# Where matmul operands start in on-chip memory: 512-byte lines for all of them, and contiguous stationary columns in the MLP

## The chip, the core and the metric

The kernel runs on one core of a Trainium2 chip. The metric is the device time of one execution in microseconds, as the median of several runs. TensorE (PE) multiplies; ScalarE (ACT) and VectorE (DVE) do the elementwise work; SyncE (SP) issues every DMA of the weights. SBUF is the on-chip memory from which TensorE reads both operands of a matmul: the stationary one (128 columns, loaded by a weight load, PEld) and the streamed one (256 or 512 columns here, read while the matmul runs).

## The reference, cut to what matters

A token stream of 256 tokens of width 1024 runs through two hybrid layers of one kind, then two of another. All arithmetic is float32.

```
# first kind, DEPTH = 2
h    = rmsnorm(x, pre_mix_g)
proj = h @ w_in                                    # 1024 -> 7440
y_a  = gated_delta_rule(conv_silu(q, k, v)) @ w_up_dn
y_b  = sliding_window_attention(...) @ w_up_sw
x    = x + rmsnorm((sigmoid(gate_a) * y_a + sigmoid(gate_b) * y_b) @ w_o, post_mix_g)
h2   = rmsnorm(x, pre_mlp_g)
x    = x + rmsnorm(square(relu(h2 @ w_ff1)) @ w_ff2, post_mlp_g)     # 1024 -> 4096 -> 1024

# second kind, DEPTH = 2, on the token stream h and a context stream hc (256 x 1024 each)
m  = silu(c) @ w_ada + b_ada                       # nine modulation rows, also for the context
h  = h + 0.5 * gate * rmsnorm(swiglu(pre(h), ffn_wi[0], ffn_wo[0]))  # 1024 -> 2 x 2816 -> 1024; also hc
o  = attention mixes of (pre(h) @ w_in) and of the context
h  = h + gate * rmsnorm(o @ w_o)                   # also hc, except in the last layer
h  = h + 0.5 * gate * rmsnorm(swiglu(pre(h), ffn_wi[1], ffn_wo[1]))  # also hc, except in the last layer
```

Nearly all of it, counted in multiplications, is the products with weights: activations (256 tokens) against weight matrices that come from HBM once.

## The kernel before, in words

Float32 accuracy is made out of a reduced float32 kind (F32R): each operand is split into a high part and the rest (`split_psum` and `wtile` do it), and each product into three matmuls into one PSUM tile, high by high, high by rest, rest by high (`mm3`, lines 262 to 268: L266, L267, L268). So the matmuls of weights come in threes, on L266, L267 and L268 in turn.

`wtile` (L237) loads a weight tile: it issues the DMAs into `raw`, ScalarE writes the high part `hi`, VectorE the rest `lo`. `hi` and `lo` are made by `shifted` (L185) in the pool `W`, in three buffers each, taken in turn; a few tiles have a buffer of their own (`hi4`, `lo4`). Each buffer is 16 elements longer than its tile.

The products run in two forms.

- **Weights stationary** (`lin_b`, L388): a weight tile of 1024 rows by 256 columns. For each stream the columns are taken in two halves of 128 and for each half the 8 blocks of rows: 2 x 8 x 3 = 48 matmuls, each with 128 stationary weight columns and 256 streamed tokens of the layer's input `xT` (`xTh` of the token stream, `xTc` of the context, both split in two). In the FFN of the second kind a weight tile serves the context and then the token stream. The program has 239 such groups of 48: 146 on `xTh`, 69 on `xTc`, 8 on `oT`, and 16 on `xTh` whose results stand in PSUM tiles called `sm`.
- **Weights streamed** (`out_mm` L1038, `lin_a` L365): 128 stationary tokens of an activation (`hid`, `mT`, `xTh`, `xTc`), and 512 columns of weights, of 4 blocks of rows at a time: groups of 12 matmuls, 306 in the program. Some products have 432 or 384 columns (288 matmuls each), and 576 matmuls stream 256 columns (`by_tokens`, L1020, at the start of the MLPs).

In the MLP of the first kind (`layer1`, from L952) the argument `turns=True` gives the hidden units an order of their own: the stationary operand of a half is every second column (`slice(j, None, 2)` in `lin_b`, L396), and the rows of `w_ff2` are loaded so that partition p holds rows 2p and 2p+1 of a pair of blocks (L255 to L257). 24 of the 239 groups are of this kind (4 plus 8 in each of two layers); `back` (L1029) reads every second column as well.

The order of all instructions is that of a recording layer with priorities; each engine runs its own list in order, and the pools' buffers say which waits there are. SyncE issues the loads of weights in their order, each when its `raw` buffer is free.

Of the kernel before, what the change touches and what calls it, by code (L numbers as in the profile page):

```python
# [9 lines left out]
F32R = mybir.dt.float32r  # L10
# [7 lines left out]
P = 128  # L18
# [4 lines left out]
EPS = 1e-6  # L23
# [9 lines left out]
TAIL = 8  # L33
# [130 lines left out]
class Kern:  # L164
    def __init__(self, tc, I, out, dbg=None):
        self.tc, self.nc, self.I, self.out, self.dbg = tc, tc.nc, I, out, dbg
        self.uid = 0
        self.flip = self.nraw = self.nw = 0
        self.deferred = []
        self.credit = self.ada_rate = 0.0  # L170

# [10 lines left out]
        kw = {} if bufs is None else {"bufs": bufs}  # L182
        return pool.tile(list(shape), dt, tag=tag, name=f"{tag}_{self.uid}", **kw)

    def shifted(self, pool, kt, n, tag, by, bufs):  # L185

        flat = self.t(pool, [P, kt * n + 16], tag, F32R, bufs=bufs)
        return flat[:, by:by + kt * n].rearrange("p (k n) -> p k n", n=n)

    def dump(self, name, ap):  # L190
# [43 lines left out]
            self.stt(lo, ps, scale, hi, ALU.mult, ALU.subtract)  # L234


    def wtile(self, parts, kt, n, own=None, turns=False):  # L237

        if own is None:
            self.nw += 1  # L240
            hi, lo = (self.shifted(self.W, kt, n, x, 0, self.w_bufs) for x in ("hi", "lo"))
        else:
            hi, lo = (self.shifted(own, kt, n, x, 0, 1) for x in ("hi4", "lo4"))
        step = 1024 // n
        for k in range(0, kt, step):
            m = min(step, kt - k)
            self.nraw += 1
            if self.raw_pool and self.nraw % 4 == 0:
                raw = self.t(self.raw_pool, [P, m, n], "raw4", bufs=1)
            else:  # L250
                raw = self.t(self.W, [P, m, n], "raw", bufs=3)
            for ap, c0 in parts:
                src = ap[k * P:(k + m) * P]
                dst = raw[:, :, c0:c0 + ap.shape[1]]
                if turns:  # L255
                    dst = dst.rearrange("p (c j) n -> p c j n", j=2)
                self.nc.sync.dma_start(out=dst, in_=src.rearrange("(c p j) n -> p c j n" if turns else "(k p) n -> p k n", p=P, **({"j": 2} if turns else {})))  # L257
            self.act(hi[:, k:k + m, :], raw)
            self.tt(lo[:, k:k + m, :], raw, hi[:, k:k + m, :], ALU.subtract)
        return hi, lo  # L260
# [124 lines left out]
                self.tick(sum(h[1] for h in held) * n)  # L385
            held = []

    def lin_b(self, parts, xs, evac, w=None, tag="mm", turns=False):  # L388


        wh, wl = w or self.wtile(parts, KB, 256)
        for key, (xh, xl) in xs:
            self.need((key, 0), (key, 1))
            ps = self.psum([P, 2, 256], tag)
            for j in range(2):
                c = slice(j, None, 2) if turns else slice(j * P, (j + 1) * P)  # L396
                for k in range(KB):
                    self.mm3(ps[:, j, :], (wh[:, k, c], wl[:, k, c]), (xh[:, k, :], xl[:, k, :]), k == 0, k == KB - 1)
            evac(key, ps)
            self.tick(16 * S)  # L400
# [35 lines left out]
    def setup(self, es):  # L436
        nc, I = self.nc, self.I

        self.t(self.pool(es, "line", side="right"), [P, 8], "line")
        self.keep = self.pool(es, "keep")  # L440
        self.small = self.pool(es, "small")
        self.cst = self.t(self.keep, [P, K_END2], "cst")
        self.cols = self.t(self.keep, [P, C_END], "cols")
        self.h = Stream("h", self.t(self.keep, [P, 2, D], "xh"))
        nc.sync.dma_start(out=self.h.x[:, 0, :], in_=I["x"][0:P, :])
        self.ident = self.cst[:, K_ID:K_ID + P]
        self.one = self.cst[:, K_ONE:K_ONE + 1]
# [415 lines left out]
    def layer1(self, l, nx, last, begin):  # L863
        nc, I = self.nc, self.I
        h = self.h
        w_in = I["w_in"][l]
        with ExitStack() as es:
            mp = self.pool(es, f"mix{l}", side="right")
            self.lay = mp
            if not begin:  # L870
                self.ada_rate = RATE1
            xh, xl = nx.x["h"]
# [3 lines left out]
            with ExitStack() as es2:  # L876
                op = self.pool(es2, f"o{l}", side="right")
                oh = self.t(op, [P, KB, S], "oT", F32R, bufs=2)
                ol = self.t(op, [P, KB, S], "oT", F32R, bufs=2)
                swt = [self.t(op, [P, 1296], "swt", bufs=2) for _ in range(2)]  # L880
                def ev(key, ps, c):
                    nc.scalar.copy(swt[key[1]][:, c * 432:(c + 1) * 432], ps)

                tiles = []
                for c, k in ((0, 0), (0, 4), (1, 0), (1, 4)):
                    w_ = self.wtile([(w_in[k * P:(k + 4) * P, 4096 + 432 * c:4528 + 432 * c], 0)], 4, 432, op if c and k else None)
# [25 lines left out]
                for c in range(4):  # L912
# [2 lines left out]
                        self.stt(s, s, 1.0, ps, ALU.add, ALU.mult)  # L915
                    self.lin_b([(I["w_up_sw"][l][:, 256 * c:256 * c + 256], 0)], [("h", (oh, ol))], ev)
            rp = self.pool(es, f"rest{l}", side="right")
            ob = [self.t(rp, [P, 8, P], "ob", bufs=2) for _ in range(2)]
            zz = [self.t(rp, [P, D], "zz", bufs=2) for _ in range(2)]
            ga = self.t(rp, [P, KB, S], "ga")  # L920
# [20 lines left out]
            for tb in range(2):  # L941
# [4 lines left out]
                s = slice(tb * P, (tb + 1) * P)  # L946
# [12 lines left out]
            nx = self.norm1(pre2)  # L959
            self.out_proj(xp, I["w_o"][l], KB, self.xs_of("h", (mh, ml)), {"h": (h, self.row_bc(I["post_mix_g"][l], xp))},  # L960
                          4 * EPS, nx)
        with ExitStack() as es:
            xh, xl = nx.x["h"]
            if l < DEPTH - 1:
                nx = self.norm1(self.row_bc(I["pre_mix_g"][l + 1], self.rowp, "gpre"))
            else:
                self.close_rows()
            mp = self.raw_pool = self.pool(es, f"ff{l}", side="right")
            self.ada_rate = 0.0
            nb = D_FF // P  # L970
# [15 lines left out]
            def unit(c, tag):  # L986
                def ev(key, ps):
                    r = relu2(ps)
                    hi, lo = place(c)
                    nc.scalar.copy(hi, r)  # L990
                    self.tt(lo, r, hi, ALU.subtract)
                self.lin_b([(w1[:, 256 * c:256 * c + 256], 0)], [("h", (xh, xl))], ev, tag=tag, turns=True)


            tiles = [self.wtile([(w1[:, 256 * c:256 * c + 256], 0)], KB, 256, mp if c == 3 else None) for c in range(FIRST)]
            for tb in range(2):
                self.need(("h", tb))
                s = slice(tb * P, (tb + 1) * P)
                for c in range(FIRST):
                    r = relu2(self.by_tokens((xh, xl), s, tiles[c]))  # L1000
                    self.back(r[:, 0, :], [x[:, :, s] for x in place(c)], turns=True)
            for c in range(FIRST, nb // 4):
                unit(c, "mm")
            xs = [(("h", tb), lambda k, tb=tb: [x[:, k % 2, tb * P:(tb + 1) * P] for x in hid[k // 2]]) for tb in range(2)]
            ps = {}
            gates = {"h": (h, self.row_bc(I["post_mlp_g"][l], mp))}
            self.ada_rate = RATE1
            self.out_head(w2, 0, nb // 2, nb, xs, ps, turns=True)
            if l == DEPTH - 1:
                nx = last()  # L1010
            self.ada_rate = 0.0
            for c in range(nb // 4, nb // 2):
                unit(c, "sm")
            self.ada_rate = RATE1
            self.out_proj(mp, w2, nb, xs, gates, EPS, nx, start=nb // 2, ps=ps, turns=True)
            self.raw_pool = self.rowp if l < DEPTH - 1 else None
        return nx

# [5 lines left out]
        self.tick(KB * 256)  # L1024
        return ps

    def back(self, r, out, turns=False):

        n = r.shape[-1] // P  # L1029
        pt = self.psum([P, n, P])  # L1030
        for j in range(n):
            self.nc.tensor.transpose(pt[:, j, :], r[:, j::n] if turns else r[:, j * P:(j + 1) * P], self.ident)
        self.split_psum(out[0], out[1], pt)

    def wrows(self, w, c, k, kt, own=None, turns=False):
        return self.wtile([(w[k * P:(k + kt) * P, c * 512:(c + 1) * 512], 0)], kt, 512, own, turns)

    def out_mm(self, ps, key, get, c, k, kt, nk, w_):  # L1038
        if (key, c) not in ps:
# [1 line left out]
        for j in range(kt):  # L1041
            self.mm3(ps[key, c], get(k + j), (w_[0][:, j, :], w_[1][:, j, :]), k + j == 0, k + j == nk - 1)

    def out_head(self, w, start, end, nk, xs, ps, k0=0, turns=False):
        for c in range(2):
            for k in range(start, end, 4):
                kt = min(4, end - k)
                w_ = self.wrows(w, c, k0 + k, kt, None, turns)
                for key, get in xs:
                    self.out_mm(ps, key, get, c, k, kt, nk, w_)  # L1050
                self.tick(kt * len(xs) * 512)

    def out_proj(self, pool, w, nk, xs, gates, eps, nx, k0=0, acc=None, tail=TAIL, start=0, ps=None, turns=False):


        head = nk - tail
        cols = [slice(c * 512, (c + 1) * 512) for c in range(2)]
        ps = {} if ps is None else ps
        self.out_head(w, start, head, nk, xs, ps, k0, turns)
        tiles = [(c, k, self.wrows(w, c, k0 + k, 4, pool if c and k > head else None, turns)) for c in range(2) for k in range(head, nk, 4)]  # L1060
# [353 lines left out]
def emit(tc, I, out, dbg=None, upto=99):  # L1414
    with ExitStack() as es:
        k = Kern(tc, I, out, dbg)
        k.setup(es)
        h = k.h
        k.xpool = k.pool(es, "xpool")
        k.W = k.pool(es, "W")  # L1420
        k.w_bufs = 3
        k.ada_pool = k.W
        es2 = ExitStack()
# [33 lines left out]
        c = k.c  # L1457
# [26 lines left out]
```

## Time and profile before

| | us |
|---|---|
| runs | 2938.57, 2940.80, 2964.28 |
| median | 2940.8 |
| the profiled execution | 2988.61 |
| its span, first to last instruction | 2986.8 |
| TensorE busy in the span | 2922.6 |
| VectorE busy | 2112.2 |
| ScalarE busy | 1319.7 |

The profiled execution is 47.8 us above the median; from 2651 to 2757 us it has TensorE at the lower of its two clocks for most of the time, which the row of the clock shows. In a timeline, each row is one instruction (or several equal ones that follow each other) with its start and its length; matmuls are pipelined, so the length of a matmul is not what it costs: that is the distance from its start to the next one's.

### The profile page before, as it was taken

What the parts mean: (1) busy time and instruction counts of PE and PEld (TensorE: products, weight loads), DVE (VectorE), ACT (ScalarE), POOL (GpSimd) and SP (SyncE); (2) the same over time, 40 slices, a digit from 0 to 9 for tenths busy, and PEclk for the clock granted to TensorE, in tenths of its full rate; (3) what the DMA queues carried; (4) which work ended last, traced back from release to release, by engine and by line L of the source; (5) the groups of instructions that cost most, each with busy time, mean ns of one, the idle gap of its engine ahead of it and who ended that gap; (6) DMA issues with size and microseconds to landing.
All of it is one profiled execution on the core that took longest, in us unless ns stands there. A gap on an engine that the chain in (4) does not pass through costs nothing.

```text
span 2986.8 us, 51176 instructions
## 1 busy us (share of the span) xinstructions
PE 2922.6 (98%) x19840; PEld 2677.3 (90%) x19840; DVE 2112.2 (71%) x5011; ACT 1319.7 (44%) x2599; POOL 0.2 (0%) x4
## 2 busy tenths in 40 slices
PE   8999999999999999999999999999999999999998
PEld 7999989789998899998978889999999999887897
DVE  7887667888867768777797769776785534663664
ACT  6555454465545454322344454322353223543543
POOL 0000000000000000000000000000000000000000
PEclk9999999999999999999999999999999999975999
DMA  6532557655235665544534224545454432330564
GB/s 221 169 100 72 162 181 227 203 157 165 75 120 159 209 194 165 149 142 137 155 113 132 81 86 142 148 146 145 128 156 142 134 94 91 92 105 11 145 189 140
DMA packets 443908, 416.76 MB, mean 140 GB/s; under 512 B 18320, under 2 KB 383760, under 8 KB 443664
## 3 DMA queue, kind: packets, MB, share of 16 engines
q1 hardware_dynamic: 443664, 413.49, 45.7%
q8 instruction: 156, 2.56, 0.4%
q14 instruction: 88, 0.72, 0.1%
HBM read 412.37 MB, written 1.05 MB: 138 GB/s over the span
## 4 chain that ended last, share of the span: by engine, by line
PE 86%; DVE 7%; DMA 4%; ACT 2%; issue 1%; SPq 0%; DVEq 0%; ACTq 0%
PE mm L267 22%; PE mm L268 22%; PE mm L266 22%; PE sm L513 4%; PE sm L561 3%; DVE lo L196 2%; PE sm L550 2%; DMA araw<-in_w_ada 2%; PE sm L794 1%; PE sm L789 1%; ACT hi L208 1%; PE sm L266 1%; PE sm L267 1%; PE sm L268 1%; DVE acc L199 1%
## 5 line engine op out<-in xcount | busy, mean ns | idle before, releaser
L196 DVE TENSOR_TENSOR lo<-raw,hi 128x1024 fp32r<-128x1024 f32 (+2 forms) x628 | 750.6, 1207 | 356.8 <-ACT hi L208 355.3
L208 ACT ACTIVATE hi<-raw 128x1024 fp32r<-128x1024 f32 (+2 forms) x628 | 646.9, 1045 | 762.2 <-PE mm L267 324.2
L267 PE MATMUL mm<-xTh,hi 128*128 128x256 f32 x2336 | 662.1, 284 | 0.8 <-DVE xTh L199 0.8
L266 PE MATMUL mm<-xTh,hi 128*128 128x256 f32 x2336 | 659.6, 283 | 3.0 <-ACT xTh L208 3.0
L268 PE MATMUL mm<-xTh,lo 128*128 128x256 f32 x2336 | 658.7, 282 | 0.0
L266 PEld LDWEIGHTS mm<-xTh,hi 128*128 128x128 f32 x2336 | 442.1, 189 | 5.0 <-ACT xTh L208 3.5
L267 PEld LDWEIGHTS mm<-xTh,hi 128*128 128x128 f32 x2336 | 442.3, 189 | 4.7 <-issue 3.3
L268 PEld LDWEIGHTS mm<-xTh,lo 128*128 128x128 f32 x2336 | 443.1, 190 | 1.4 <-issue 1.3
L199 DVE SCALAR_TENSOR_TENSOR acc<-araw,csil,acc 128x256 f32<-128x256 f32 x896 | 391.2, 479 | 71.8 <-DMA araw<-in_w_ada 69.2
L266 PE MATMUL mm<-hi,hid 128*128 128x512 f32 x872 | 344.4, 395 | 0.0
L267 PE MATMUL mm<-lo,hid 128*128 128x512 f32 x872 | 343.6, 394 | 0.0
L268 PE MATMUL mm<-hi,hid 128*128 128x512 f32 x872 | 343.5, 394 | 0.0
L266 PE MATMUL mm<-xTc,hi 128*128 128x256 f32 x1104 | 310.7, 281 | 0.0
L267 PE MATMUL mm<-xTc,hi 128*128 128x256 f32 x1104 | 309.7, 281 | 0.0
L268 PE MATMUL mm<-xTc,lo 128*128 128x256 f32 x1104 | 308.1, 279 | 0.9 <-DVE lo L196 0.9
L268 PEld LDWEIGHTS mm<-xTc,lo 128*128 128x128 f32 x1104 | 208.3, 189 | 1.1 <-DVE lo L196 1.1
L267 PEld LDWEIGHTS mm<-xTc,hi 128*128 128x128 f32 x1104 | 208.1, 189 | 0.7 <-issue 0.3
L266 PEld LDWEIGHTS mm<-xTc,hi 128*128 128x128 f32 x1104 | 207.4, 188 | 0.4
L268 PEld LDWEIGHTS mm<-hi,hid 128*128 128x128 f32 x872 | 164.5, 189 | 37.4
L267 PEld LDWEIGHTS mm<-lo,hid 128*128 128x128 f32 x872 | 164.1, 188 | 37.0
L266 PEld LDWEIGHTS mm<-hi,hid 128*128 128x128 f32 x872 | 163.9, 188 | 37.0
L266 PE MATMUL mm<-hi,xTh 128*128 128x256 f32 (+3 forms) x512 | 180.4, 354 | 4.4 <-ACT xTh L1143 3.3
(315 smaller groups left out, 4689.1 us busy)
## 6 DMA issues: line engine op xcount, KB each, us to landing
raw<-in_ffn_wi SPq DMA_DIRECT2D x352, 256.0 KB, 3.8
araw<-in_w_ada SPq DMA_DIRECT2D x288, 256.0 KB, 3.0
raw<-in_w_ff SPq DMA_DIRECT2D x128, 512.0 KB, 4.3
raw<-in_w_in SPq DMA_DIRECT2D x116, 512.0 KB, 3.9
raw<-in_ffn_wo SPq DMA_DIRECT2D x88, 512.0 KB, 4.1
raw<-in_w_o SPq DMA_DIRECT2D x40, 512.0 KB, 3.4
raw<-in_w_in SPq DMA_DIRECT2D x24, 432.0 KB, 4.5
raw<-in_w_up_sw SPq DMA_DIRECT2D x16, 512.0 KB, 3.6
```

Of the source, the lines that this page charges most:

```text
L196: self.nc.vector.tensor_tensor(out=out, in0=a, in1=b, op=op)
L199: self.nc.vector.scalar_tensor_tensor(out=out, in0=a, scalar=s, in1=b, op0=op0, op1=op1)
L208: self.nc.scalar.activation(out, a, func, **kw)
L266: mm(ps, lhsT=ah, rhs=bh, start=first, stop=False)
L267: mm(ps, lhsT=ah, rhs=bl, start=False, stop=False)
L268: mm(ps, lhsT=al, rhs=bh, start=False, stop=last)
L513: nc.tensor.matmul(ps[:, h, o:o + n], lhsT=q, rhs=k, start=True, stop=True)
L550: nc.tensor.transpose(ps[:, b, :], sc[:, b // nb, (b % nb) * P:(b % nb + 1) * P], self.ident)
L561: nc.tensor.matmul(po[:, h, :], lhsT=pT[:, h * nb + kb, :], rhs=v, start=kb == 0, stop=kb == nb - 1)
L789: nc.tensor.matmul(ps[:, i, :], lhsT=LT[:, i, :], rhs=Dm[:, i, :], start=True, stop=True)
L794: nc.tensor.matmul(ps[:, i, :], lhsT=DT[:, i, :], rhs=M[:, i, :], start=True, stop=True)
```

## The change

Five things.

1. `shifted` places a tile by what it is: the streamed kind (more than 256 columns) at the start of its buffer, the stationary kind with `hi` 48 elements (192 bytes) in and `lo` 96 elements (384 bytes) in. Each buffer is 128 elements (512 bytes) longer than its tile, not 16.
2. The pools `xpool` (layer inputs) and `W` are opened ahead of the others, and padding tiles called `line` are put into several pools, so that these pools and many tiles start at multiples of 512 bytes.
3. `turns` goes: in the MLP the stationary operand is 128 neighbouring columns.
4. With it, partition p of a block of `w_ff2` gets row p of that block, as everywhere else.
5. The counter `nw`, which nothing read, goes.

The memory map of the two built programs gives these offsets, in bytes, of the operands' starts within a 512-byte line (every block of rows lies a multiple of 512 bytes further on, so one number stands for all):

```
operand                                         before                      after
stationary hi / lo, by buffer (lin_b)           0/192, 64/256, 128/320      192/384 in all three
  the same, in buffers of their own             320/384                     192/384
streamed xTh (lin_b)                            0                           0
streamed xTc (lin_b)                            384                         0
streamed oT (lin_b)                             128                         0
stationary step between columns, MLP            8 bytes                     4 bytes
streamed hi / lo, by buffer (512 columns)       0/192, 64/256, 128/320      0/0
  the same, in buffers of their own             320/384                     0/0
stationary hid (512 columns)                    448                         0
stationary xTh / xTc / mT (512 columns)         0 / 384 / 192               0 / 0 / 0
```

The groups that the rows below begin with: the weight tile multiplied at 1210.78 and 1216.47 us has `hi` at 0 (buffer of `lo` at 192), the one at 1278.19 and 1283.84 at 128, the one at 1289.50 and 1295.05 at 64; the one at 505.98 us at 64. Of the groups of 12, the streamed `hi` lies at 64 from 1365.51 us, at 0 from 1368.29, at 128 from 1379.49 and at 0 from 1782.89 us.

Every engine's list holds the same instructions in the same order in both programs: 18,844 entries on TensorE, 5,884 on VectorE, 3,018 on ScalarE, 2,014 on SyncE. No wait differs but one: on SyncE the load of the context's first half into `xc` (L1444) now waits for a matmul of the last delta-rule group (a count of TensorE that L840 reaches), seven counts after the one that the load before it already waits for. Only addresses, steps and the rows' places in the loads of `w_ff2` differ.

```diff
-    def shifted(self, pool, kt, n, tag, by, bufs):
+    def shifted(self, pool, kt, n, tag, bufs):
-        flat = self.t(pool, [P, kt * n + 16], tag, F32R, bufs=bufs)
+        by = 0 if n > 256 else 48 if tag[:2] == "hi" else 96
+        flat = self.t(pool, [P, kt * n + 128], tag, F32R, bufs=bufs)
         return flat[:, by:by + kt * n].rearrange("p (k n) -> p k n", n=n)
...
         if own is None:
-            self.nw += 1
-            hi, lo = (self.shifted(self.W, kt, n, x, 0, self.w_bufs) for x in ("hi", "lo"))
+            hi, lo = (self.shifted(self.W, kt, n, x, self.w_bufs) for x in ("hi", "lo"))
         else:
-            hi, lo = (self.shifted(own, kt, n, x, 0, 1) for x in ("hi4", "lo4"))
+            hi, lo = (self.shifted(own, kt, n, x + "4", 1) for x in ("hi", "lo"))
...
-                dst = raw[:, :, c0:c0 + ap.shape[1]]
-                if turns:
-                    dst = dst.rearrange("p (c j) n -> p c j n", j=2)
-                self.nc.sync.dma_start(out=dst, in_=src.rearrange("(c p j) n -> p c j n" if turns else "(k p) n -> p k n", p=P, **({"j": 2} if turns else {})))
+                self.nc.sync.dma_start(out=raw[:, :, c0:c0 + ap.shape[1]], in_=src.rearrange("(k p) n -> p k n", p=P))
...
-                c = slice(j, None, 2) if turns else slice(j * P, (j + 1) * P)
+                c = slice(j * P, (j + 1) * P)
...
-        self.t(self.pool(es, "line", side="right"), [P, 8], "line")
+        self.t(self.pool(es, "line", side="right"), [P, 120], "line")
+        self.t(self.pool(es, "line2"), [P, 96], "line")
+        self.xpool = self.pool(es, "xpool")
+        self.W = self.pool(es, "W")
         self.keep = self.pool(es, "keep")
+        self.t(self.keep, [P, 32], "line")
...
             mp = self.pool(es, f"mix{l}", side="right")
             self.lay = mp
+            self.t(mp, [P, 112], "line")
...
+                self.t(op, [P, 96], "line")
...
             rp = self.pool(es, f"rest{l}", side="right")
+            self.t(rp, [P, 112], "line")
...
-            self.nc.tensor.transpose(pt[:, j, :], r[:, j::n] if turns else r[:, j * P:(j + 1) * P], self.ident)
+            self.nc.tensor.transpose(pt[:, j, :], r[:, j * P:(j + 1) * P], self.ident)
...
-        k.xpool = k.pool(es, "xpool")
-        k.W = k.pool(es, "W")
```

## Rows read from the trace of the kernel before

**Rows 1.** The page: TensorE's row of busy time, and its clock by slices.

```profile
PE 2922.6 (98%) x19840; PEld 2677.3 (90%) x19840; DVE 2112.2 (71%) x5011; ACT 1319.7 (44%) x2599; POOL 0.2 (0%) x4
PEclk9999999999999999999999999999999999975999
```

**Rows 2.** The page: the chain of work that ended last, by engine.

```profile
PE 86%; DVE 7%; DMA 4%; ACT 2%; issue 1%; SPq 0%; DVEq 0%; ACTq 0%
```

**Rows 3.** Waits of TensorE: total us, times, longest; the longest of twenty.

```profile
PE sm L408 <- DVE xn L203: 19.8, 5, 10.9
```

**Rows 4.** Groups by line and form: count | busy us, mean ns | idle before.

```profile
L266 PE MATMUL mm<-xTh,hi 128*128 128x256 f32 x2336 | 659.6, 283 | 3.0 <-ACT xTh L208 3.0
L266 PE MATMUL mm<-xTc,hi 128*128 128x256 f32 x1104 | 310.7, 281 | 0.0
L266 PE MATMUL mm<-hi,hid 128*128 128x512 f32 x872 | 344.4, 395 | 0.0
```

**Rows 5.** Timeline, FFN of two streams: first matmuls of groups of 48 (start, length).

```profile
1210.78 0.28 PE L266 MATMUL mm<-xTc,hi 128*128 128x256 f32 x1
1216.47 0.28 PE L266 MATMUL mm<-xTh,hi 128*128 128x256 f32 x1
...
1278.19 0.28 PE L266 MATMUL mm<-xTc,hi 128*128 128x256 f32 x1
1283.84 0.28 PE L266 MATMUL mm<-xTh,hi 128*128 128x256 f32 x1
1289.50 0.28 PE L266 MATMUL mm<-xTc,hi 128*128 128x256 f32 x1
...
1294.82 0.28 PE L267 MATMUL mm<-xTc,hi 128*128 128x256 f32 x1
1294.93 0.28 PE L268 MATMUL mm<-xTc,lo 128*128 128x256 f32 x1
1295.05 0.28 PE L266 MATMUL mm<-xTh,hi 128*128 128x256 f32 x1
...
1300.70 0.28 PE L266 MATMUL mm<-xTc,hi 128*128 128x256 f32 x1
```

**Rows 6.** Timeline, MLP of the first layer: first matmuls of groups with every second column.

```profile
505.98 0.28 PE L266 MATMUL sm<-xTh,hi 128*128 128x256 f32 x1
...
511.74 0.28 PE L266 MATMUL sm<-xTh,hi 128*128 128x256 f32 x1
```

**Rows 7.** Timeline, streamed weights: first matmuls of one, four and four groups of 12.

```profile
1365.51 0.39 PE L266 MATMUL mm<-hi,hid 128*128 128x512 f32 x1
...
1368.29 0.40 PE L266 MATMUL mm<-hi,hid 128*128 128x512 f32 x1
...
1379.49 0.39 PE L266 MATMUL mm<-hi,hid 128*128 128x512 f32 x1
...
1390.49 0.28 PE L266 MATMUL mm<-xTc,hi 128*128 128x256 f32 x1
```

**Rows 8.** The same view: one group of 12 with stationary `xTh`, streamed `hi` at 0.

```profile
1782.89 0.40 PE L266 MATMUL mm<-hi,xTh 128*128 128x512 f32 x1
1785.65 0.39 PE L266 MATMUL mm<-hi,xTh 128*128 128x512 f32 x1
```

**Rows 9.** Stretches: us, busy us (instructions) of PE, PEld, DVE, ACT, POOL, clock, DMA.

```profile
1010.00:1048.00 38.00, 38.00 (x166) 30.89 (x165) 36.12 (x67) 14.09 (x15) 0.00 (x0) 1.00 0.81 260
2651.10:2757.00 105.90, 104.47 (x373) 82.43 (x371) 34.70 (x132) 34.08 (x107) 0.00 (x0) 0.53 0.06 18
```

**Rows 10.** Timeline of SyncE's queue: the context's load and the next load of weights.

```profile
872.26 0.43 SPq L1444 DMA_DIRECT2D xc<-in_ctx  x1
876.80 0.38 SPq L257 DMA_DIRECT2D raw<-in_w_in  x1
```

**Rows 11.** The page, issues of DMAs: count, KB each, us to landing.

```profile
raw<-in_w_ff SPq DMA_DIRECT2D x128, 512.0 KB, 4.3
raw<-in_w_in SPq DMA_DIRECT2D x116, 512.0 KB, 3.9
```

More of the change, by code (lines that the diff above doesn't have):

```diff
@@ L167, in __init__ @@
         self.uid = 0
-        self.flip = self.nraw = self.nw = 0
+        self.flip = self.nraw = 0
         self.deferred = []
@@ L234, in split_psum, with wtile @@
             self.stt(lo, ps, scale, hi, ALU.mult, ALU.subtract)
-    def wtile(self, parts, kt, n, own=None, turns=False):
+    def wtile(self, parts, kt, n, own=None):
         if own is None:
-            self.nw += 1
-            hi, lo = (self.shifted(self.W, kt, n, x, 0, self.w_bufs) for x in ("hi", "lo"))
+            hi, lo = (self.shifted(self.W, kt, n, x, self.w_bufs) for x in ("hi", "lo"))
         else:
-            hi, lo = (self.shifted(own, kt, n, x, 0, 1) for x in ("hi4", "lo4"))
+            hi, lo = (self.shifted(own, kt, n, x + "4", 1) for x in ("hi", "lo"))
         step = 1024 // n
@@ L386, in lin_a, with lin_b @@
             held = []
-    def lin_b(self, parts, xs, evac, w=None, tag="mm", turns=False):
+    def lin_b(self, parts, xs, evac, w=None, tag="mm"):
         wh, wl = w or self.wtile(parts, KB, 256)
@@ L991, in ev @@
                     self.tt(lo, r, hi, ALU.subtract)
-                self.lin_b([(w1[:, 256 * c:256 * c + 256], 0)], [("h", (xh, xl))], ev, tag=tag, turns=True)
+                self.lin_b([(w1[:, 256 * c:256 * c + 256], 0)], [("h", (xh, xl))], ev, tag=tag)
             tiles = [self.wtile([(w1[:, 256 * c:256 * c + 256], 0)], KB, 256, mp if c == 3 else None) for c in range(FIRST)]
@@ L1000, in layer1 @@
                     r = relu2(self.by_tokens((xh, xl), s, tiles[c]))
-                    self.back(r[:, 0, :], [x[:, :, s] for x in place(c)], turns=True)
+                    self.back(r[:, 0, :], [x[:, :, s] for x in place(c)])
             for c in range(FIRST, nb // 4):
@@ L1007, in layer1 @@
             self.ada_rate = RATE1
-            self.out_head(w2, 0, nb // 2, nb, xs, ps, turns=True)
+            self.out_head(w2, 0, nb // 2, nb, xs, ps)
             if l == DEPTH - 1:
@@ L1014, in layer1 @@
             self.ada_rate = RATE1
-            self.out_proj(mp, w2, nb, xs, gates, EPS, nx, start=nb // 2, ps=ps, turns=True)
+            self.out_proj(mp, w2, nb, xs, gates, EPS, nx, start=nb // 2, ps=ps)
             self.raw_pool = self.rowp if l < DEPTH - 1 else None
@@ L1025, in by_tokens, with back @@
         return ps
-    def back(self, r, out, turns=False):
+    def back(self, r, out):
         n = r.shape[-1] // P
@@ L1031, in back, with wrows @@
         for j in range(n):
-            self.nc.tensor.transpose(pt[:, j, :], r[:, j::n] if turns else r[:, j * P:(j + 1) * P], self.ident)
+            self.nc.tensor.transpose(pt[:, j, :], r[:, j * P:(j + 1) * P], self.ident)
         self.split_psum(out[0], out[1], pt)
-    def wrows(self, w, c, k, kt, own=None, turns=False):
-        return self.wtile([(w[k * P:(k + kt) * P, c * 512:(c + 1) * 512], 0)], kt, 512, own, turns)
+    def wrows(self, w, c, k, kt, own=None):
+        return self.wtile([(w[k * P:(k + kt) * P, c * 512:(c + 1) * 512], 0)], kt, 512, own)
     def out_mm(self, ps, key, get, c, k, kt, nk, w_):
@@ L1042, in out_mm, with out_head @@
             self.mm3(ps[key, c], get(k + j), (w_[0][:, j, :], w_[1][:, j, :]), k + j == 0, k + j == nk - 1)
-    def out_head(self, w, start, end, nk, xs, ps, k0=0, turns=False):
+    def out_head(self, w, start, end, nk, xs, ps, k0=0):
         for c in range(2):
@@ L1047, in out_head @@
                 kt = min(4, end - k)
-                w_ = self.wrows(w, c, k0 + k, kt, None, turns)
+                w_ = self.wrows(w, c, k0 + k, kt)
                 for key, get in xs:
@@ L1051, in out_head, with out_proj @@
                 self.tick(kt * len(xs) * 512)
-    def out_proj(self, pool, w, nk, xs, gates, eps, nx, k0=0, acc=None, tail=TAIL, start=0, ps=None, turns=False):
+    def out_proj(self, pool, w, nk, xs, gates, eps, nx, k0=0, acc=None, tail=TAIL, start=0, ps=None):
         head = nk - tail
@@ L1058, in out_proj @@
         ps = {} if ps is None else ps
-        self.out_head(w, start, head, nk, xs, ps, k0, turns)
-        tiles = [(c, k, self.wrows(w, c, k0 + k, 4, pool if c and k > head else None, turns)) for c in range(2) for k in range(head, nk, 4)]
+        self.out_head(w, start, head, nk, xs, ps, k0)
+        tiles = [(c, k, self.wrows(w, c, k0 + k, 4, pool if c and k > head else None)) for c in range(2) for k in range(head, nk, 4)]
         for key, get in xs:
```

## The prediction

> **What bounds the kernel now.** I read the page's busy times first. TensorE is busy 2922.6 of 2986.8 us, VectorE 71% [rows 1], and the chain of work that ended last runs through TensorE for 86% [rows 2]. The list of what TensorE waited for says the same from the other side: its longest entry is 19.8 us, nearly all at the start [rows 3]. So a time that each matmul saves is a time that the kernel saves, unless another engine steps in. [...]
>
> Then I looked at what a matmul costs, by the distance between starts. A group of 48 (16 steps of three, one 256-column weight tile on one stream) is the unit, and the timeline shows each group's first matmul [rows 5]. No group shown waits for anything, and the clock is full. Yet they differ by their operands' places:
>
> - on `xTc` (at 384) with `hi` at 0: 1210.78 to 1216.47, 5.69 us
> - on `xTc` with `hi` at 128: 1278.19 to 1283.84, 5.65; on `xTh` (at 0) with the same tile: 5.66
> - on `xTc` with `hi` at 64: 1289.50 to 1295.05, **5.55**; on `xTh` with the same tile: 5.65
>
> The last pair says most: the same weights in the same buffer, one stream after the other, 0.10 us apart. So neither the buffer nor the weights' offset alone decides; the distance between stationary and streamed operand may. In the fast pair `hi` lies 64 - 384 = 192 bytes behind the streamed operand (modulo 512) and `lo` 256 - 384 = 384. **The change puts every group at just this distance**: `hi` at 192, `lo` at 384, all streamed inputs at 0. In the MLP with every second column a group takes 505.98 to 511.74, 5.76 [rows 6].
>
> **The change, part by part.**
>
> *Groups of 48.* There are 239: the counts on L266, 2336 on `xTh` and 1104 on `xTc` [rows 4], are 146 and 69 groups of 16 steps; 16 more stand in `sm`, 8 on `oT`. I take 5.55 for all of them afterwards.
> - 24 with every second column: 24 x (5.76 - 5.55) = 5.0 us.
> - 144 contiguous ones on `xTh` and `oT` (146 + 16 + 8 - 24, less 2 on `oT` that have the good distance modulo 256): 144 x (5.655 - 5.55) = 15.1 us.
> - On `xTc`, the three buffers come in turn, 22 groups each, and 3 have buffers of their own. At 64: nothing. At 0: 22 x (5.69 - 5.55) = 3.1. At 128 and the three: 25 x (5.65 - 5.55) = 2.5.
>
> Together 25.7 us. Nothing in the profile shows `hi` at 192 with the stream at 0, so bounds. At best every step would be as short as the two that end the fast group, 1294.82 to 1295.05 for two [rows 5], 48 x 0.115 = 5.52 a group: 239 x 0.03 = 7 us more, 33 in all. At worst every group costs what the worst row shows, 5.76: 144 x 0.105 + 22 x 0.07 + 25 x 0.11 + 24 x 0.21 = 24 us more than now. I take 5.55 because its row has the same distances.
>
> *Groups of 12 with streamed weights.* 306 of them (872 steps on `hid` [rows 4], 352 on the others, four steps a group). With `hid` at 448 they take 2.78 us with `hi` at 64 (1365.51 to 1368.29), 11.20 / 4 = 2.80 at 0, and 11.00 / 4 = 2.75 at 128 [rows 7]: 2.777 on average. Afterwards both operands start at 0. The nearest row has stationary `xTh` at 0 and streamed `hi` at 0 (only `lo` elsewhere): 1782.89 to 1785.65, 2.76 [rows 8]. I take that: 306 x 0.017 = 5.2 us. Ends: 2.75 (8 us less) and 2.80 (7 us more). The 1152 matmuls of other widths I leave as they are; they change in both directions by a digit's worth.
>
> *Contiguous columns.* They are in the 24 groups above. [...]
>
> *Loads of `w_ff2`.* The bytes of each piece stay the same, and only the rows' partitions change. `w_ff` tiles land in 4.3 us, the `w_in` tiles, loaded the plain way, in 3.9 [rows 11]. While `w_ff2` streams, TensorE is busy 38.00 of 38.00 us [rows 9], so 0.4 us either way is hidden by matmuls, three `raw` buffers deep. Without that cover it would be 64 x 0.4 = 26 us at most, in either direction; I take 0.
>
> *The added wait.* The load of `xc` was issued at 872.26 us; the next load on SyncE's queue went out at 876.80, held by its own buffer [rows 10]. The new wait ends seven TensorE counts after one that the queue passes anyway, within the gap of 4.5 us. Those 4.5 us cover it: 0, and some 1 us if not. What is queued behind it is that load of weights.
>
> *Padding and pools.* No instruction, no other wait: 0.
>
> *Sum:* 25.7 + 5.2 = 30.9 us. TensorE is busy 98% of the span, so I let 2% of that be lost in places where it waits anyway: 30. Profiled: 2988.6 - 30 = 2959 with the same dip; against the median, 2940.8 - 30 = **2911 us**, 1.0% faster.
>
> **The rivals.**
>
> *A. Places don't matter.* Then the 5.55 groups are an accident of the `xTc` stretches, and only the contiguous columns count: 24 x 0.1 = 2.4 us, 2938 us. For it speaks that the offsets are an inference from the memory map. Against it: 22 groups, each third one on `xTc`, in a fixed rotation, and the second stream with the same tile at 5.65 [rows 5]. [...] Chance 0.14.
>
> *B. The time comes back as waits.* VectorE is at 36.12 of 38.00 us in the `w_ff2` stretch [rows 9], and SyncE's loads wait for buffers that VectorE frees. If TensorE's groups shorten and half of the gain is lost to a late `lo`, 2940.8 - 15 = 2926. Against it: over the whole span VectorE is at 71% [rows 1], and the saving is 2% of a group. Chance 0.12.
>
> *C. Slower: one line for all.* All streams and all weights now start on the same offsets, and the distance is not what counts but where the stream itself starts: `xTc` leaves 384, where the best groups were, for 0, where none of `xTh`'s was good, and streamed weights meet their stationary operand on one line. Then all groups cost 5.76 (24 us more) and groups of 12 cost 2.80 (7 us more): 2940.8 + 31 = 2972. It decides from 5.68 a group upwards, and is a slowdown over 1% from about 5.75. For it: `xTh` at 0 shows no group under 5.65 [rows 5]. Against it: contiguous groups at 0 show none over 5.66 either. Chance 0.07.
>
> *D. The change doesn't do what it says:* the built program's map shows the offsets, so this has no chance worth a number.
>
> **How the numbers follow.** My forecast has 0.67, with its own range of 2900 to 2922 (the groups of 48 between 5.52 and 5.59, those of 12 between 2.75 and 2.775). A measurement of this kernel tells a change from none at about 1%, here 2911.4, which cuts the forecast in two: I give 0.40 to faster and 0.27 to within 1%. A and B are within 1%: 0.27 + 0.14 + 0.12 = 0.53. C is slower: 0.07. The range takes in B and nearly all of A and leaves out C: below, 2896 the best ends of both terms together (33 + 8 = 41 us, 2900) and a little more; above, 2940. Some 0.16 is left out.
>
> **What would show it.** In the changed profile, groups of 48 on `xTh` and on `xTc` should be alike, 5.55 us from first start to first start, all three buffers, and in the MLP too; the mean length of L266 to L268 rows on `xTh` should fall by about 2 ns. Groups of 12 should take 2.76. Order and waits stay. Groups still at 5.65 would make A right; equal groups at 5.55 with new waits before L267 or L268 on `lo` would make B right; 5.76 makes C right. I would be wrong by more than the range if the offset of the stream itself, not the distance, set the time of a group.

## The result, and the profile after

Over 20 runs each, the changed kernel has a median of 2923.61 us (2904.68 to 2954.69) and the kernel before 2962.48 us (2936.46 to 2984.34). The ratio is **0.9883, 95% interval 0.9853 to 0.9914**: 1.2% faster, clear of noise. The median before lies higher than that of the three runs shown. The runs differ in their mean granted clock (of the changed kernel, from 0.994 at 2904.68 us to 0.977 at 2954.69), and the ratio is of the means of the runs within 1.5% of the fastest of their kernel (17 of the changed one, 19 of the one before); the two fastest are 31.8 us apart. 0.9883 x 2940.8 = 2906 us stands beside the forecast of 2911.

The profiled execution of the changed kernel took 2933.71 us. Its page: busy time, clock by slices, and the chain by engine.

```profile
span 2931.9 us, 51176 instructions
PE 2863.6 (98%) x19840; PEld 2636.8 (90%) x19840; DVE 2110.2 (72%) x5011; ACT 1320.1 (45%) x2599; POOL 0.2 (0%) x4
PEclk9999999999999999999999999999999999987999
PE 85%; DVE 7%; DMA 4%; ACT 3%; issue 2%; SPq 0%; DVEq 0%; ACTq 0%
```

TensorE lost 59 us of busy time against [rows 1]; VectorE and ScalarE did the same work. Part of the 59 us is the clock. The stretch at the lower clock, a granted 0.50 near the end, is shorter here, 58.2 us against 105.9 (columns as in [rows 9]):

```profile
2619.50:2677.70 58.20, 56.79 (x206) 45.89 (x205) 19.77 (x72) 18.76 (x59) 0.00 (x0) 0.50 0.10 32
```

By an estimate from the 0.50, it would have been half as long at full clock, 29 us less: 2933.7 - 29 = 2905. The same estimate for the profile of before, whose 105.9 us have a mean of 0.53 [rows 9], is 0.47 x 105.9 = 50 us less: 2988.6 - 50 = 2939, near the median of its three runs. So the two profiles, freed of that stretch, are 34 us apart, as the ratio has it. One stretch shows what the lower clock cost: the same 166 matmuls took 51.77 us at 0.50 in the profile of before (2704.67 to 2756.44) and 27.74 us at 1.00 in this one (2677.66 to 2705.40), 1.87 times as long; with 1.87 in place of 2 the profiles are 36 us apart.

Where they came from shows in the starts of the groups. First matmuls of groups of 48 in the changed kernel's timeline (L264 to L266 are now the three matmuls of a step), the same places as in [rows 5] and [rows 6]:

```profile
1198.15 0.28 PE L264 MATMUL mm<-xTc,hi 128*128 128x256 f32 x1
1203.69 0.28 PE L264 MATMUL mm<-xTh,hi 128*128 128x256 f32 x1
...
1264.34 0.28 PE L264 MATMUL mm<-xTc,hi 128*128 128x256 f32 x1
1269.89 0.28 PE L264 MATMUL mm<-xTh,hi 128*128 128x256 f32 x1
1275.43 0.28 PE L264 MATMUL mm<-xTc,hi 128*128 128x256 f32 x1
1280.98 0.28 PE L264 MATMUL mm<-xTh,hi 128*128 128x256 f32 x1
...
501.43 0.28 PE L264 MATMUL sm<-xTh,hi 128*128 128x256 f32 x1
506.97 0.28 PE L264 MATMUL sm<-xTh,hi 128*128 128x256 f32 x1
```

Each is 5.54 or 5.55 us behind the one before it, on either stream and in the MLP, where the last pair took 5.76 before. A group that can be read alone has no other matmul between its 48, runs at full clock, and doesn't start right behind a matmul of another kind with a first step of some 0.2 us; these are 183 of the 239. Of them 178 took 5.55 to 5.58 us. The other five follow each other without a pause, at the same offsets, and took 5.65. One of them:

```profile
684.18 0.28 PE L264 MATMUL mm<-oT,hi 128*128 128x256 f32 x1
689.83 0.28 PE L264 MATMUL mm<-xTh,hi 128*128 128x256 f32 x1
```

So a group at the good distance can also run in a slower rhythm; the experiments come back to it. Groups of 12 with streamed weights, the places of [rows 7] and [rows 8]:

```profile
1352.94 0.39 PE L264 MATMUL mm<-hi,hid 128*128 128x512 f32 x1
...
1363.82 0.39 PE L264 MATMUL mm<-hi,hid 128*128 128x512 f32 x1
...
1374.69 0.28 PE L264 MATMUL mm<-xTc,hi 128*128 128x256 f32 x1
...
1764.26 0.39 PE L264 MATMUL mm<-hi,xTh 128*128 128x512 f32 x1
1766.98 0.39 PE L264 MATMUL mm<-hi,xTh 128*128 128x512 f32 x1
```

Four groups take 10.88 and 10.87 us, 2.72 each, and the one on `xTh` 2.72. That is below the best row of before (2.75).

Because both programs have the same list, every matmul can be set beside itself. The distances from each start to the next, without the stretches at the lower clock in either profile, add up like this (us; in the last row TensorE stood idle before the next matmul):

```
                                        count    before     after   difference
groups of 48, contiguous                10259    1222.1    1204.1      -18.0
the same, every second column before     1126     135.1     130.4       -4.6
groups of 12, streamed weights           3626     846.5     831.8      -14.7
all other matmuls                        4213     552.6     551.6       -1.1
TensorE idle before the next               59      53.7      57.2       +3.5
```

The waits of TensorE, longest first (total, times, longest), are those of [rows 3] with little more on them:

```profile
PE sm L405 <- DVE xn L205: 21.0, 5, 11.1
PE sm L1138 <- DVE xn L205: 9.0, 7, 2.4
```

### The profile page after: what moved, and what is told of

Its sections match the earlier page's. It is cut to its first block, busy times and chain, and to the rows that moved or that the text cites. A ratio compares the mean times of both kernels' runs of the same rounds, so it can differ in the third digit from the quotient of the medians.

```text
span 2931.9 us, 51176 instructions
## 1 busy us (share of the span) xinstructions
PE 2863.6 (98%) x19840; PEld 2636.8 (90%) x19840; DVE 2110.2 (72%) x5011; ACT 1320.1 (45%) x2599; POOL 0.2 (0%) x4
## 4 chain that ended last, share of the span: by engine, by line
PE 85%; DVE 7%; DMA 4%; ACT 3%; issue 2%; SPq 0%; DVEq 0%; ACTq 0%
PE mm L265 22%; PE mm L264 22%; PE mm L266 22%; PE sm L514 3%; PE sm L562 3%; DVE lo L198 2%; PE sm L551 2%; DMA araw<-in_w_ada 1%; PE sm L795 1%; DVE acc L201 1%; PE sm L790 1%; ACT hi L210 1%; PE sm L264 1%; PE sm L265 1%; PE sm L266 1%
## 5 line engine op out<-in xcount | busy, mean ns | idle before, releaser
L264 PE MATMUL mm<-xTh,hi 128*128 128x256 f32 x2336 | 656.5, 281 | 3.0 <-ACT xTh L210 3.0
L266 PE MATMUL mm<-xTh,lo 128*128 128x256 f32 x2336 | 650.6, 279 | 0.0
L264 PEld LDWEIGHTS mm<-xTh,hi 128*128 128x128 f32 x2336 | 438.8, 188 | 5.0 <-ACT xTh L210 3.5
L266 PEld LDWEIGHTS mm<-xTh,lo 128*128 128x128 f32 x2336 | 438.9, 188 | 1.4 <-issue 1.3
L264 PE MATMUL mm<-hi,hid 128*128 128x512 f32 x872 | 340.7, 391 | 0.0
L266 PE MATMUL mm<-hi,hid 128*128 128x512 f32 x872 | 340.0, 390 | 0.0
L264 PE MATMUL mm<-xTc,hi 128*128 128x256 f32 x1104 | 308.9, 280 | 0.0
L266 PE MATMUL mm<-xTc,lo 128*128 128x256 f32 x1104 | 305.3, 277 | 1.1 <-DVE lo L198 1.1
L266 PEld LDWEIGHTS mm<-xTc,lo 128*128 128x128 f32 x1104 | 206.5, 187 | 1.3 <-DVE lo L198 1.3
L264 PEld LDWEIGHTS mm<-xTc,hi 128*128 128x128 f32 x1104 | 206.6, 187 | 0.3
L266 PEld LDWEIGHTS mm<-hi,hid 128*128 128x128 f32 x872 | 164.0, 188 | 34.3
L264 PEld LDWEIGHTS mm<-hi,hid 128*128 128x128 f32 x872 | 164.0, 188 | 33.2
L264 PE MATMUL mm<-hi,xTh 128*128 128x256 f32 (+3 forms) x512 | 178.3, 350 | 4.4 <-ACT xTh L1147 2.8
```

The costliest lines, as they stand in the source:

```text
L264: mm(ps, lhsT=ah, rhs=bh, start=first, stop=False)
L266: mm(ps, lhsT=al, rhs=bh, start=False, stop=last)
```

## The experiments

All are the changed kernel with one thing moved. Each profile gives the time of groups; the timed ratio is to the kernel before, where the changed kernel has 0.9883.

**The columns.** The MLP's stationary operand is every second column again; the rows of `w_ff2` and `back` go with it. At the lines of the old diff:

```diff
-                c = slice(j * P, (j + 1) * P)
+                c = slice(j, None, 2) if turns else slice(j * P, (j + 1) * P)
```

> The changed kernel with the old MLP columns back (every second column stationary, w_ff2 rows in the old places), all offsets as changed. Distance theory (the distance between stationary and streamed operand sets a matmul's time) with the step between columns as a cost of its own: the 24 groups of 48 with every second column take 5.65 us (the 0.10 us that the step cost before, on top of 5.55), so 2.4 us more in all; the others stay at 5.55. Rival, offsets alone: the 24 groups take 5.55 as well and the time is the changed kernel's. Groups of 12 at 2.72 in both.

Measured: ratio 0.9864 (0.9797 to 0.9931), fastest run 2908.35 us against 2904.68. Two first matmuls of such groups:

```profile
504.29 0.28 PE L267 MATMUL sm<-xTh,hi 128*128 128x256 f32 x1
510.08 0.28 PE L267 MATMUL sm<-xTh,hi 128*128 128x256 f32 x1
```

5.79 us, against 5.55 contiguous at the same offsets. All 21 of them that can be read alone took 5.79 or 5.80. The step between columns has a price, 0.24 us a group or 24 x 0.24 = 5.8 us, more than the 0.10 of before: at the better distance there is more to lose. In the total it is within the interval; the rows settle it. The sums of the two lists differ by 5.6 us over these groups.

**Another distance.** `hi` at 0, `lo` at 192:

```diff
-        by = 0 if n > 256 else 48 if tag[:2] == "hi" else 96
+        by = 0 if n > 256 else 0 if tag[:2] == "hi" else 48
```

> The changed kernel with the stationary weights moved to 0 (hi) and 192 bytes (lo) in their lines; they stay contiguous, streams stay at 0. Distance theory: all 239 groups of 48 take the 5.66 us that this distance took before (hi at 0, lo at 192, stream at 0), 239 x 0.11 = 26 us more than the changed kernel; groups of 12 stay at 2.72. Rival, alignment of buffers alone (equal buffers, padded pools): groups stay at 5.55 and the time is the changed kernel's.

Measured: ratio 0.9940 (0.9893 to 0.9988). Groups on `xTc` and `xTh`:

```profile
1268.16 0.28 PE L264 MATMUL mm<-xTc,hi 128*128 128x256 f32 x1
1273.81 0.28 PE L264 MATMUL mm<-xTh,hi 128*128 128x256 f32 x1
1279.47 0.28 PE L264 MATMUL mm<-xTc,hi 128*128 128x256 f32 x1
```

5.65 or 5.66 each, on all 183 groups read alone (5.651 to 5.658); with the same offsets one took 5.66 before (from 1216.47 us). Alignment as such gives the groups of 48 nothing; half of the change's gain is in the 192 bytes. What is left, 0.6%, is groups of 12 (2.72 as in the changed kernel) and contiguous columns.

**The same distance elsewhere.** One padding tile grows by 128 bytes, and with it move the layer inputs and all weights:

```diff
-        self.t(self.pool(es, "line2"), [P, 96], "line")
+        self.t(self.pool(es, "line2"), [P, 128], "line")
```

> The changed kernel with one padding tile 128 bytes longer, which moves the layer inputs and all weights by 128 bytes together: hi at 320, lo at 0, inputs at 128; streamed weights at 128 too, while hid stays at 0. Distance theory: groups of 48 on xTh and xTc stay at 5.55, since the distances (192 and 384) stay. Rival, place theory (the stream must start a 512-byte line): they go to about 5.65, 24 us more. Groups of 12 on hid: 2.72 if what counts is that the distance is the same for all three matmuls of a step; 2.75 to 2.80 if both operands must start on the same offset; those on xTh and xTc (both at 128) stay at 2.72 by the distance.

Measured: ratio 0.9946 (0.9898 to 0.9994). Groups of 48, four groups of 12 on `hid`, and one on `xTh`:

```profile
1272.87 0.28 PE L264 MATMUL mm<-xTc,hi 128*128 128x256 f32 x1
1278.41 0.28 PE L264 MATMUL mm<-xTh,hi 128*128 128x256 f32 x1
1283.96 0.28 PE L264 MATMUL mm<-xTc,hi 128*128 128x256 f32 x1
...
1361.96 0.40 PE L264 MATMUL mm<-hi,hid 128*128 128x512 f32 x1
...
1373.11 0.39 PE L264 MATMUL mm<-hi,hid 128*128 128x512 f32 x1
...
1772.78 0.39 PE L264 MATMUL mm<-hi,xTh 128*128 128x512 f32 x1
1775.50 0.40 PE L264 MATMUL mm<-hi,xTh 128*128 128x512 f32 x1
```

Groups of 48 on `xTh` and `xTc` stay at 5.54 and 5.55, with a stream that starts at 128 (five in a row in the second layer's MLP took 5.65, and six whose weights have buffers of their own, which did not move, have `hi` 64 and `lo` 256 behind the stream and took 5.66): the distance decides, not the 512-byte line. The eight groups on `oT`, which stays at 0, got another distance, `hi` 320 behind the stream and `lo` at 0. Six of these can be read alone: two took 5.65, and four in a row took 5.86 or 5.87, more than any group in the surveys below:

```profile
110.56 0.28 PE L264 MATMUL mm<-oT,hi 128*128 128x256 f32 x1
116.42 0.28 PE L264 MATMUL mm<-oT,hi 128*128 128x256 f32 x1
```

Groups of 12 say the same with both outcomes in one run: on `xTh`, 128 behind 128, 2.72; on `hid`, streamed at 128 against 0, 11.15 / 4 = 2.79. So it isn't enough that the distance stays the same from matmul to matmul; distance 0 is the good one. The sums have 15 us lost on groups of 12, nearly all of them on `hid`: most of this kernel's distance from the changed one.

**Distance 0 for all.**

```diff
-        by = 0 if n > 256 else 48 if tag[:2] == "hi" else 96
+        by = 0
```

> The changed kernel with all weights at 0 of their lines, hi and lo alike, so that every matmul of a step has the same distance, 0. If a distance that does not change from matmul to matmul is what made the groups of 12 faster than foreseen (2.72 against 2.76), the groups of 48 profit as well: 48 x 0.113 = 5.42 us, 239 x 0.13 = 31 us less than the changed kernel. If each distance has its own price (steps from 0 to 0 took 119 ns in groups of 48 before), they take 48 x 0.119 = 5.7 us, 36 us more. Groups of 12 at 2.72 in both.

Measured: ratio 0.9997 (0.9955 to 1.0038).

```profile
1277.80 0.28 PE L264 MATMUL mm<-xTc,hi 128*128 128x256 f32 x1
1283.56 0.28 PE L264 MATMUL mm<-xTh,hi 128*128 128x256 f32 x1
1289.32 0.28 PE L264 MATMUL mm<-xTc,hi 128*128 128x256 f32 x1
```

5.76 us. The distance that is best for 512 columns is among the worst for 256, and it gives back all the change had won: 239 x 0.21 = 50 us lost on groups of 48, by the sums 44.6. This is also what the prediction's rival C priced, 5.76 a group: a layout "on whole lines" alone lands there.

**Surveys.** The offset is drawn from a list, so that one run holds all pairs (here in steps of 64 bytes, a second run in steps of 32):

```diff
-        by = 0 if n > 256 else 48 if tag[:2] == "hi" else 96
+        which = n > 256
+        if tag[:2] == "hi":
+            self.places[which] += 1
+        i = self.places[which]
+        by = 16 * ((i if tag[:2] == "hi" else i // 8 + i) % 8)
```

> The changed kernel with each weight tile at another pair of places: hi at 0, 64, ... 448 in turn, lo 0, 64, ... 448 behind it, all 64 pairs, the streamed weights likewise; inputs and stationary activations stay at 0. Only the times of single groups are read. Distance theory: groups of 48 with (hi, lo) at (192, 384) take 5.55, at (0, 192) 5.66, at (0, 0) 5.76; pairs that differ by 256 in both agree, as before ((64, 256) after a stream at 384 and at 128 took the same). Groups of 12 at (0, 0) take 2.72, at (0, 192) 2.76 and at constant 128 (stationary 384 ahead) 2.79. If some pair makes every step 113 ns, its groups take 5.42. Rival, history theory (what decides is the order of tiles and how the loads before it left the two reads): equal pairs take different times in different places.

Measured, mean us of a group of 48 by how far `hi` (down) and `lo` (across) lie behind the stream, 183 groups:

```
hi \ lo      0     64    128    192    256    320    384    448
    0    5.749  5.667  5.719  5.653  5.753  5.668  5.717  5.653
   64    5.648  5.655  5.678  5.478  5.650  5.655  5.675  5.460
  128    5.676  5.654  5.697  5.603  5.678  5.654  5.697  5.604
  192    5.652  5.440  5.559  5.656  5.652  5.440  5.564  5.655
  256    5.756  5.655  5.717  5.655  5.753  5.654  5.718  5.655
  320    5.652  5.552  5.674  5.454  5.656  5.519  5.676  5.455
  384    5.677  5.652  5.696  5.603  5.677  5.654  5.694  5.602
  448    5.652  5.441  5.572  5.655  5.654  5.450  5.565  5.655
```

The lower half repeats the upper one and the right half the left one, but for two entries ((320, 64) and (320, 320), 5.552 and 5.519 where 5.655 is expected): the period for these groups is 256 bytes, not 512. The two entries are means of two times: three of their seven groups took 5.656, four 5.44 to 5.46. The pair of the change, (192, 384), is the third best kind. (192, 64) and (64, 192) are better, and need no more memory. For groups of 12, (0, 0) was best of all pairs at 2.73, (0, 192) took 2.75 and constant 128 took 2.79, about as expected. The history theory has something as well: these two entries show groups of one pair that differ by 0.2 us.

> The survey again in steps of 32 bytes, hi and lo at 0 to 224 (all 64 pairs); only the times of single groups are read. Distance theory with a period of 256 bytes: the pairs in multiples of 64 repeat the first survey, 5.44 at (192, 64), 5.55 at (192, 128), 5.76 at (0, 0); between them values between, or lower ones if the best distance is no multiple of 64. Rival, a price that goes in steps of 64 bytes: neighbours 32 apart take the same.

Measured: no pair of the finer grid that isn't in the coarse one has a mean under 5.633. Neighbours 32 bytes apart differ (5.46 at (64, 192), 5.66 at (64, 160) and at (64, 224)), so the price doesn't go in steps of 64. But (192, 64) showed two times in this run: 5.44 to 5.45 twice, 5.703 twice.

> The survey with the rest of the layer input moved: its high part at 0, its rest at 0, 64, 128 or 192 in turn by layer part, hi and lo of the stationary weights in 16 pairs of 0 to 192; streamed weights at 0. Only the times of single groups are read. If each matmul's price is that of its own distance and the next load's, moving the rest changes the second of three matmuls alone, and for some pair all three take 113 ns: 5.42 a group. If the streamed operand's start matters only to its own matmul, pairs with the rest at 0 repeat the first survey.

Here the input's rest, which the second matmul of a step streams, was at 0, 64, 128 or 192, by this in `Norm` and for the output of the delta rule:

```diff
+        flats = [self.t(pool, [P, KB * S + 128], tag, F32R, bufs=2) for _ in range(2)]
+        return [f[:, by:by + KB * S].rearrange("p (k n) -> p k n", n=S) for f, by in zip(flats, (0, 16 * (self.npair % 4)))]
```

With the rest at 0 the pairs repeat the first survey (5.44 at (192, 64), 5.46 at (64, 192), 5.75 at (0, 0)), but for (64, 64), where three groups of four took 5.46 or 5.47 and not 5.66. With the rest elsewhere no pair has a mean under 5.56, and the 5.42 foreseen came with none. So the best pairs took their 5.44 and 5.46 only with both streams at the same start.

**Two candidates.**

```diff
-        by = 0 if n > 256 else 48 if tag[:2] == "hi" else 96
+        by = 0 if n > 256 else 48 if tag[:2] == "hi" else 16
```

> The changed kernel with one number moved: stationary lo at 64 bytes of its line instead of 384, hi stays at 192. Distance theory, with the survey's 5.440 us for hi 192 and lo 64 behind the stream: all 239 groups of 48 take 5.44 instead of 5.55, 26 us less than the changed kernel, ratio to the kernel before about 0.979 to 0.980. Groups of 12 stay at 2.72. Rival, waits (the engines that feed TensorE have no more room): groups at 5.44 but waits that grow by ten us or more, ratio about 0.984 to 0.988.

Measured: ratio 0.9827 (0.9784 to 0.9870). Of 183 groups, 139 took 5.44 or 5.45, and 44 took 5.71. Two groups of the same lines in the first layer and in the second:

```profile
498.92 0.28 PE L264 MATMUL sm<-xTh,hi 128*128 128x256 f32 x1
...
504.36 0.28 PE L264 MATMUL sm<-xTh,hi 128*128 128x256 f32 x1
...
1063.41 0.28 PE L264 MATMUL sm<-xTh,hi 128*128 128x256 f32 x1
...
1069.11 0.28 PE L264 MATMUL sm<-xTh,hi 128*128 128x256 f32 x1
```

5.44 and 5.70, with the same offsets and no wait in either. In the fast ones the steps are 113, 113 and 114 ns; in the slow ones 117 to 119, with 124 or 125 every sixth matmul, all through the group and through the groups that follow without a pause. So the distance leaves two rhythms, and in this profile a group kept the one it started in. The rival didn't stand: TensorE's idle time fell, from 68.3 to 65.3 us. The second rhythm, which neither theory had, took more than half of the 26 us (the groups of 48 gained 10.0 by the sums).

```diff
-        by = 0 if n > 256 else 48 if tag[:2] == "hi" else 96
+        by = 0 if n > 256 else 16 if tag[:2] == "hi" else 48
```

> The changed kernel with stationary hi at 64 and lo at 192 bytes of their lines; streams stay at 0. In the surveys this pair took 5.44 to 5.50 us a group of 48 whatever went before it, where (192, 64) took 5.44 or 5.71 by what went before. Distance theory: 239 x (5.55 - 5.46) = 21 us less than the changed kernel, ratio to the kernel before about 0.981, and no group over 5.52. Rival, a second slower rhythm as with (192, 64): part of the groups at 5.65 or more, and a gain of 10 us or less.

Measured: ratio **0.9802** (0.9745 to 0.9860), fastest run 2883.73 us.

```profile
1255.35 0.28 PE L264 MATMUL mm<-xTc,hi 128*128 128x256 f32 x1
1260.79 0.28 PE L264 MATMUL mm<-xTh,hi 128*128 128x256 f32 x1
1266.23 0.28 PE L264 MATMUL mm<-xTc,hi 128*128 128x256 f32 x1
```

All 183 groups read alone took 5.44 to 5.48, so no second rhythm showed in this profile.

> The changed kernel as it is, for a comparison on the same chip: ratio to the kernel before 0.985 to 0.991, groups of 48 at 5.55, groups of 12 at 2.72.

Measured beside it: 0.9862 (0.9810 to 0.9914), fastest run 2905.84 us; groups of 48 at 5.55 but for ten, of 12 at 2.72. The intervals of the two versions overlap; the matmuls tell them apart. Set beside itself, each matmul counted, the version with (64, 192) saves 25.2 us on groups of 48, TensorE stands idle 3 us longer (69.5 against 66.3), and the fastest runs are 22 us apart. So it is the fastest of the layouts tried.

The ten groups took 5.65. Five are those that took it in the first profile of this kernel; the other five are in the second layer's MLP, where the same groups took 5.55 then. One group in the first profile, and the same one in this:

```profile
1069.15 0.28 PE L264 MATMUL sm<-xTh,hi 128*128 128x256 f32 x1
1074.70 0.28 PE L264 MATMUL sm<-xTh,hi 128*128 128x256 f32 x1
...
1065.09 0.28 PE L264 MATMUL sm<-xTh,hi 128*128 128x256 f32 x1
1070.74 0.28 PE L264 MATMUL sm<-xTh,hi 128*128 128x256 f32 x1
```

5.55 and 5.65 in two executions of one program, with no wait in either: offsets cannot make this difference. At one distance the time of a group is one of two, and something that differs from execution to execution (or, as far as these two can tell, from chip to chip) can choose between them.

## Why the prediction was right, and where it was off

The sign, the mechanism and the total held: 30 us forecast, 34 by the two profiles, and the ratio's interval is 25 to 43 us of 2940.8. That the total is this close is in part luck: one term was some 3 us too large, one 9.5 too small, and more came back in waits than was put aside. No run shows the 2959 of a profiled execution "with the same dip": the stretch at the lower clock was 58.2 us long in the changed kernel's profile, not 105.9, and the execution took 2933.71.

- *Groups of 48, 25.7 us.* Right to the row for 178 of the 183 groups read alone; five took 5.65. By the matched matmuls it is 22.6 us over 11,385 of the 11,472. The groups without other matmuls between theirs gained 0.107 us each, 20.6 us for 192 of them; the 47 others, which the sum counted at the same price, gained some 2 us. That the distance between the operands decides was an inference from one row in three; the runs with another distance (5.65) and with the same distance elsewhere (5.55) show it. The prediction's own rows had a sign that it isn't all: 5.69 (stream at 384, `hi` at 0) and 5.66 (stream at 0, `hi` at 128) are one distance, 128 for `hi` and 320 for `lo`. Of the 51 contiguous groups at that distance that can be read alone in the profile before, 32 took 5.64 to 5.66 and 19 took 5.69 or 5.70, some of either on both streams.
- *Contiguous columns.* Shown: 5.79 against 5.55 at equal offsets, where the sum had 0.21 a group from both causes together.
- *Groups of 12, 5.2 us.* **The mis-sized term.** I took 2.76 from the nearest row, which had `hi` at distance 0 and `lo` at 192, and set the lower end at 2.75. With both at 0 they take 2.72: 306 x 0.057 = 17 us by the rows, 14.7 us by the 3626 matched matmuls. In the nearest row the starts are 228 to 230 ns apart once the group is under way, behind `lo` as behind `hi`; with both at 0 it is 226 to 227. So a step with one operand at another distance was slower as a whole, and the row could not show what the good distance gives when all three have it.
- *Waits.* Kept at 2% of the gain, some 0.6 us. The matched matmuls with TensorE idle behind them took 3.5 us longer, and its idle time went from 2986.8 - 2922.6 = 64.2 to 2931.9 - 2863.6 = 68.3 us, so some 4 us came back: rival B, at a quarter of its price. With 22.6 + 14.7 + 1.1 - 3.5 = 34.9 us the sum closes on the measured 34.
- *The added wait.* `xc` went out at 865.41 us, 1.68 behind the load ahead of it instead of 0.39; the next load left at 868.68, 3.27 us later and held by its own buffer. Nothing, as priced:

```profile
863.73 0.34 SPq L429 DMA_DIRECT2D gbc<-in_post_mix_g  x1
865.41 0.34 SPq L1446 DMA_DIRECT2D xc<-in_ctx  x1
868.68 1.62 SPq L255 DMA_DIRECT2D raw<-in_w_in  x2
```

- *Loads of `w_ff2`.* `w_ff` tiles land in 4.2 us where they took 4.3 [rows 11], and TensorE is busy 37.00 of 37.00 us in that stretch. Nothing, as priced:

```profile
1001.00:1038.00 37.00, 37.00 (x165) 30.65 (x164) 35.02 (x66) 14.52 (x15) 0.00 (x0) 1.00 0.80 255
```

And its row among the page's DMA issues (issue to landing last):

```profile
raw<-in_w_ff SPq DMA_DIRECT2D x128, 512.0 KB, 4.2
```

- *Rival A* (places don't matter) fell: four layouts of the same instructions take 5.44, 5.55, 5.65 and 5.76 a group. *Rival C*'s price was real and its place wrong: 5.76 is what distance 0 costs streams of 256 columns; the change doesn't put them there.
- *The chances.* With the second term at its true size the forecast would have been 2898 to 2900 before what waits take back, well past the 1% bound, and faster would have had more than 0.40.

## What to carry to other kernels

Where TensorE is the bound (98% busy here) and streams are short (256 and 512 columns here), compare groups of equal matmuls by the distance of their starts before looking at anything else. Two levels in one program, with no wait, came here from the operands' places (5.55 and 5.65 us in [rows 5]) and, at one place, from the rhythm a group ran in (5.44 and 5.70 at (192, 64)); several executions and several groups at each place tell which. Then let one run try all places, since buffers can take another offset each, and read the price from the groups, each group and not only the mean. Check that the best place is fast everywhere in the program and not in one of two rhythms.

## What the runs showed of the hardware that was not expected

- The price of a matmul depends on how far its stationary and its streamed operand lie apart in SBUF, in the survey with a period of 256 bytes for 48 matmuls of 256 columns (5.749 us at (0, 0), 5.753 at (0, 256) and 5.756 at (256, 0); two of the 64 pairs did not repeat). The means of the pairs of both surveys are 5.44 to 5.77 us (113 to 120 ns a matmul), and four groups of one run took 5.86 or 5.87; 12 of 512 columns took 2.72 to 2.81 us. Why is not shown by any run.
- The best distance for 512 columns, 0 (2.72 us for 12), is among the worst for 256 (5.76 us for 48, against 5.44 at (64, 192)).
- At some distances a group takes one of two times, each with its own rhythm: 5.44 and 5.71 us a group at (192, 64), 5.55 and 5.65 at (192, 384), 5.65 and 5.70 at (128, 320), 5.44 to 5.46 and 5.66 at (320, 64), 5.65 and 5.87 at (320, 0). At (64, 192) and at (0, 192) one run each at that distance throughout showed only one, 5.44 to 5.48 and 5.65 to 5.66. Groups that followed without a pause at (192, 64) kept the rhythm; two executions of one program chose differently for five groups. What sets the rhythm a group starts in stays open.
- Reading every second column as the stationary operand cost 0.24 us in 48 matmuls at (192, 384), 5.79 against 5.55.
